# A streaming encoder layer: output products take the PSUM bank released longest ago, and the last but one row tile is scaled around the last add

## The chip, the cores and the metric

The kernel runs on one core of a Trainium2 chip. The core has five engines that run side by side, each with its own queue of instructions, done in order: TensorE (PE in the profile, with its weight loads as PEld), VectorE (DVE), ScalarE (ACT), GpSimd (POOL) and SyncE (SP, which here only issues DMAs). Matmuls write into PSUM, which is cut into banks; VectorE and ScalarE read the banks and so empty them. The metric is the device time of one execution in microseconds (us), as the median of several runs; lower is better.

## What is computed

One inference step of a hybrid encoder with one layer: 2048 prompt frames of one stream and 64 frames of a running stream, width 1024. The input is normalised and projected by one matrix into an attention part and a gated recurrent part. Their outputs stand side by side (`mix`, 1024 wide) and go through the output projection, the residual add and a last RMSNorm. The change touches only this end:

```python
y = x + jnp.concatenate([o_a, o_b], axis=-1) @ w_out   # mixer_layer
...
y_prompt = rms_norm(hp, ln_f_g)
y_sample = rms_norm(hs, ln_f_g)
```

`rms_norm(x, g)` is x times 1/sqrt(mean(x*x) + 1e-6) of its row, times g.

## The kernel before

**Tiles.** The 2048 prompt rows are worked through in four stretches of 512 (`SUPER`; the second has the 64 running frames as well). For each, the 32 column tiles of the input projection are multiplied (`project`), and attention and recurrence work on what comes out. Their result is written to DRAM (`mixd`). At the end comes the output projection. It takes 256 rows at a time: a **pair** of two row tiles of 128 (tile 0 and tile 1), eight pairs, numbered 0 to 7. Each row tile has two halves of 512 columns.

**Products.** For a pair, the product of 256 x 1024 by 1024 x 1024 is done with a Strassen-like scheme of 7 products (`NPROD`) of blocks of 128 rows by 512 by 512. Operands are split into a high and a low part, so each product is 12 matmuls of 128 x 512 into one PSUM bank: for each of 4 blocks of the inner dimension high by high, low by high, high by low (`out_step`, matmuls issued by the helper `mm` at line 249). The left operand of a product is made in `out_parts` (line 1751, ScalarE: the high part) and `out_low` (line 1759, VectorE, for pairs 0 and 1 mostly GpSimd: the low part); it lies in a `slot`, or in a part of `xh` and `xl`, which serve as a fifth slot. The sums of blocks that later products need are made at lines 1772 and 1777. The right operand, the weights, lies in memory that other stages have left: product 0 in `b11h`, `b11l`; 1 and 2 in `w`; 3 and 4 in `xh`, `xl`; 5 in `kd`, `q`, `ql`; 6 in `ph`, `v`. So a matmul's row in the profile tells its product: `acc<-w,slot` is product 1 or 2, written to the bank `acc`.

**Adds.** When a product is done, `out_adds` empties its bank. Products 0, 2 and 4 go also into a running sum `u` (`reset` or `asb`; ScalarE at line 1865, VectorE at line 1873). `ADDS` lists to which half of which tile a product is added; `out_add` does it on VectorE (line 1847), and for the sums `u` on GpSimd (line 1852). The tiles hold the residual x beforehand, in whatever buffer is free: `xn`, `bias`, two `pr`, or `rest` and `sga`. For pair 7, tile 0 is `bias` and tile 1 is two `pr`. Product 6 is added to half 0 of tile 1 alone, and it is the last add of a pair.

**Norm.** When a half has had its last add, `out_norm` squares and sums it (ScalarE, line 1896). The first half of a tile leaves its sum (line 1903), the second completes it (lines 1915 and 1916: the row factor `rstd`). Then the tile is multiplied by `rstd` and the gain `g_in` and goes out by DMA: in most tiles in one instruction (lines 1921, 1924), else by halves (lines 1937, 1940). For pair 7's tile 1 one half has been multiplied by the gain ahead (line 1909), so that ScalarE can scale it (1928, DMA at 1929) while VectorE scales the other (1931, DMA at 1932).

**Order.** Nothing on the chip chooses the order. At build time a planner (`Plan`) runs a clock of its own with estimated durations; each piece of work is a generator that yields what it waits for (a time, a free engine, a condition), and instructions get into the engines' queues in the order in which the generators go on. Tokens (`Tok`, in `tk`) count buffers: each holds planned release times; `n` is how many lie in the past, `take` removes the earliest, `when` tells it. The real waits for data and buffers are semaphores that are put in from the tiles that instructions use.

**Banks.** `out_bank` picks the bank of a product: `acc` (two buffers) or `g` (one), and when attention is over (`late`) also `tr` (two) and `pv` (one). Before the change it takes the first tag in this order that has a released buffer; the buffers of one tag are taken in turn.

## Time and profile before

| | |
|---|---|
| median of 3 runs | 1247.02 us (1246.3 to 1247.69) |
| the profiled execution | 1245.85 us, of which its span (first to last instruction) is 1244.1 us |
| PE busy | 1229.7 us of the span |
| DVE, ACT, POOL busy | 897.0, 680.6, 415.2 us |
| granted TensorE clock, mean | 0.998 |
| output stage without attention beside it | about 1098 us to the end |

How to read it: the profile page gives sums and shares; views of the trace give single instructions. A row of the timeline has start, duration, engine, line, operation, output<-inputs, shape, count, and in brackets how long the engine was idle just before it and what ended that. A row of the waits names who waited for whom, with total, count and longest. A row of the windows has the stretch, its length, the busy time of PE, PEld, DVE, ACT and POOL, the granted clock, the DMA engines' busy share and GB/s. Matmuls are pipelined: a matmul's duration is longer than the distance to the next one's start.

### The profile page before, as it was taken

What the parts mean: (1) busy time and instruction counts of PE and PEld (TensorE: products, weight loads), DVE (VectorE), ACT (ScalarE), POOL (GpSimd) and SP (SyncE); (2) the same over time, 40 slices, a digit from 0 to 9 for tenths busy, and PEclk for the clock granted to TensorE, in tenths of its full rate; (3) what the DMA queues carried; (4) which work ended last, traced back from release to release, by engine and by line L of the source; (5) the groups of instructions that cost most, each with busy time, mean ns of one, the idle gap of its engine ahead of it and who ended that gap; (6) DMA issues with size and microseconds to landing.
All of it is one profiled execution on the core that took longest, in us unless ns stands there. A gap on an engine that the chain in (4) does not pass through costs nothing.

```text
span 1244.1 us, 21258 instructions
## 1 busy us (share of the span) xinstructions
PE 1229.7 (99%) x7398; PEld 1078.0 (87%) x7398; DVE 897.0 (72%) x1897; ACT 680.6 (55%) x1526; POOL 415.2 (33%) x702
## 2 busy tenths in 40 slices
PE   9999999999999999999999999999999999999997
PEld 7888888999999999998888888988888888778785
DVE  7697878867767677786577667775768666867774
ACT  6354545754656556574465656664646445644433
POOL 7665564111120110201233242143252203665453
PEclk9999999999999999999999999999999999999999
DMA  8897888667575575655787778678888776976431
GB/s 338 302 322 258 320 297 324 204 184 255 155 217 148 158 248 189 203 164 187 276 272 247 277 265 280 226 254 264 262 280 244 238 243 208 366 243 213 144 118 68
DMA packets 158324, 294.36 MB, mean 237 GB/s; under 512 B 51657, under 2 KB 98377, under 8 KB 140554
## 3 DMA queue, kind: packets, MB, share of 16 engines
q1 hardware_dynamic: 157784, 292.74, 70.3%
q8 instruction: 58, 0.95, 0.3%
q14 instruction: 48, 0.39, 0.1%
q10 hardware_dynamic: 434, 0.27, 0.1%
HBM read 198.52 MB, written 95.49 MB: 236 GB/s over the span
## 4 chain that ended last, share of the span: by engine, by line
PE 87%; DMA 4%; DVE 4%; issue 2%; ACT 2%; POOL 1%; SPq 0%; DVEq 0%; POOLq 0%; ACTq 0%
PE acc L249 62%; PE g L249 7%; PE pv L249 6%; PE tr L253 5%; PE s L249 5%; DMA w<-wd 1%; DMA out_dram<-ck 1%; DMA way<-vT 1%; POOL sig L1777 1%; DMA vT<-way 1%; DMA mixd<-ob 1%; PE g L253 1%; DMA mixd<-mixa 0%; DMA bias<-wind 0%; DVE xn L1847 0%
## 5 line engine op out<-in xcount | busy, mean ns | idle before, releaser
L249 PE MATMUL acc<-xh,w 128*128 128x512 f32 (+2 forms) x2720 | 564.3, 347 | 0.7 <-ACT xh L409 0.5
L249 PEld LDWEIGHTS acc<-xh,w 128*128 128x128 f32 x2720 | 435.5, 189 | 51.5 <-ACT xh L409 0.9
L249 PE MATMUL acc<-xl,w 128*128 128x512 f32 (+2 forms) x1360 | 291.3, 346 | 0.4 <-DVE xl L415 0.4
L249 PEld LDWEIGHTS acc<-xl,w 128*128 128x128 f32 x1360 | 220.5, 189 | 26.3 <-DVE xl L415 0.6
L948 DVE CUSTOM_DVE_ANT_0 pr<-s,bias 128x640 f32<-128x640 f32 (+4 forms) x128 | 94.2, 736 | 52.1 <-PE s L249 51.6
L965 ACT ACTIVATE pr<-pr,nm 128x640 f32<-128x640 f32 (+4 forms) x132 | 100.3, 760 | 52.4 <-DVE nm L948 52.1
L977 ACT CAST ph<-tr 128x512 fp32r<-128x512 f32 (+3 forms) x176 | 87.8, 506 | 74.1 <-PE pv L249 45.2
L473 POOL TENSOR_TENSOR w<-wraw,w 128x256 fp32r<-128x256 f32 x120 | 102.3, 882 | 55.2 <-DVE w L468 43.2
L980 DVE TENSOR_TENSOR ph<-tr,ph 128x512 fp32r<-128x512 f32 (+3 forms) x176 | 100.8, 588 | 21.5 <-ACT ph L977 20.9
L249 PE MATMUL pv<-ph,v 128*128 128x256 f32 (+2 forms) x344 | 97.7, 370 | 0.8 <-DVE ph L980 0.5
L253 PE MATMUL tr<-ident,pr 128*128 128x128 f32 x580 | 88.3, 273 | 0.0
L1596 POOL TENSOR_TENSOR k<-ob 128x512 f32<-128x512 f32 (+2 forms) x20 | 18.0, 902 | 200.7 <-ACT ob L1587 161.7
L1121 POOL TENSOR_TENSOR mixa<-mixa,sga 128x256 f32<-128x256 f32 (+1 forms) x36 | 28.5, 793 | 167.8 <-DVE mixa L1019 154.2
L510 POOL TENSOR_TENSOR xn<-wraw,xn 128x256 fp32r<-128x256 f32 x48 | 40.2, 838 | 132.7 <-ACT xn L507 132.7
L969 DVE TENSOR_SCALAR pr<-pr,sm 128x640 f32<-128x640 f32 (+4 forms) x132 | 76.2, 577 | 4.7
L1019 DVE TENSOR_TENSOR mixa<-mixa,pv 64x256 f32<-64x256 f32 (+1 forms) x144 | 56.8, 395 | 31.0 <-ACT mixa L1015 27.3
L253 PEld LDWEIGHTS tr<-ident,pr 128*128 128x128 f32 x580 | 69.6, 140 | 10.0 <-DVE ph L980 0.8
L575 ACT ACTIVATE sig<-acc 128x512 f32<-128x512 f32 (+2 forms) x63 | 31.8, 505 | 72.2 <-PE acc L249 71.6
L249 PEld LDWEIGHTS pv<-ph,v 128*128 128x128 f32 (+1 forms) x344 | 58.3, 189 | 9.5 <-DVE ph L980 1.2
L1015 ACT COPY mixa<-pv 64x256 f32<-64x256 f32 (+1 forms) x72 | 25.1, 349 | 59.2 <-PE pv L249 53.4
L249 PE MATMUL s<-kd,q 128*128 128x320 f32 (+2 forms) x232 | 55.9, 311 | 0.2 <-DVE nm L948 0.2
L249 PE MATMUL s<-kd,ql 128*128 128x320 f32 (+2 forms) x232 | 55.5, 309 | 0.0
(343 smaller groups left out, 2124.1 us busy)
## 6 DMA issues: line engine op xcount, KB each, us to landing
w<-wd SPq DMA_DIRECT2D x96, 1024.0 KB, 5.9
wd<-w SPq DMA_DIRECT2D x32, 1024.0 KB, 7.0
wraw<-in_w_in_dram SPq DMA_DIRECT2D x30, 512.0 KB, 5.4
wod<-xn SPq DMA_DIRECT2D x28, 512.0 KB, 5.7
xn<-in_x_prompt_dram SPq DMA_DIRECT2D x23, 512.0 KB, 4.6
bias<-biasd SPq DMA_DIRECT2D x24, 320.0 KB, 5.7
carry<-kd SPq DMA_DIRECT2D x12, 512.0 KB, 6.6
carry<-v SPq DMA_DIRECT2D x12, 512.0 KB, 6.6
```

The source lines that it names most:

```text
L249: pe.matmul(out, w, x, **kw)
L253: pe.transpose(out, x, idn)
L473: pool.tensor_sub(w[:, 1, k : k + 2], raw[:, k : k + 2], f32(w[:, 0, k : k + 2]))
L510: pool.tensor_sub(f32r(st[:, c.start + 512 : c.stop + 512]), src[:, c], st[:, c])
L575: act.activation(sig[:, :bn], acc, AF.Exp, scale=-1.0)
L948: dve.tensor_tensor_reduce(s[:, :nk].rearrange("p (a c) -> p a c", a=ns), sps[:, :ns, :kn], d.bias[:, h, bcol : bcol + nk].rearrange("p (a ...
L965: act.activation(s[:, :nk], s[:, :nk], AF.Exp, bias=nm[:, 0:1], scale=-1.0, accum_out=sm)
L969: dve.tensor_scalar(s[:, :nk], s[:, :nk], sm, None, ALU.mult)
L977: act.copy(ph[:krows, 0, :wid], pt[:krows, :wid])
L980: dve.tensor_sub(ph[:krows, 1, :wid], pt[:krows, :wid], f32(ph[:krows, 0, :wid]))
L1019: dve.tensor_add(mix[hs, :qn], mix[hs, :qn], pv[hs, i, :qn])
L1121: pool.tensor_mul(mix[:, :n], mix[:, :n], d.sg[:, g0 : g0 + n])
```

## The change

Two things. First, `out_bank` takes, of the tags that have a released buffer, the one whose buffer was released earliest by the planner's times, in place of the first in a fixed order. Second, for the last add of all (pair 7, product 6) `out_adds` waits until the first half of tile 0 has been scaled, and the scaling of tile 0's second half waits until that add has been issued, in place of waiting for a planned time; in both halves the DMA is issued to SP's queue at once.

```diff
@@ out_bank
-        tag = [x for x in some if tk[x].n][0]
+        tag = min((x for x in some if tk[x].n), key=lambda x: tk[x].when())
@@ out_adds
+        closing = i == len(pairs) - 1 and k == NPROD - 1
         for tile_, half in ADDS[k]:
+            if closing:
+                yield lambda: "scaled0" in o
             t = yield from out_add(o, tile_, half, bank[1], t)
+        if closing:
+            o["added"] = True
@@ out_norm
                 c = slice(a * 512, a * 512 + 512)
-                yield "D", t
+                if end and a:
+                    yield lambda: "added" in o
+                else:
+                    yield "D", t
                 dve.scalar_tensor_tensor(x[a][:rows], x[a][:rows], r[:rows], g_in[:rows, c], ALU.mult, ALU.mult)
                 t = C.dve(530, t)
-                yield t
+                if end:
+                    o["scaled0"] = True
+                else:
+                    yield t
                 sp.dma_start(y[:, c], x[a][:rows])
```

## The prediction

> **What bounds the kernel.** First the page: which engine is full.

> ```profile
> PE 1229.7 (99%) x7398; PEld 1078.0 (87%) x7398; DVE 897.0 (72%) x1897; ACT 680.6 (55%) x1526; POOL 415.2 (33%) x702
> ```

> TensorE is busy 99% of the span, so an edit that touches no matmul can only win back holes in its row and the stretch behind its last matmul. The first part of the change deals with the PSUM bank that an output product takes, so I ask the waits of PE from 1098 us, where attention has ended, to 1236 us, the last matmul.

> ```profile
> PE acc L249 <- DVE pr L1847: 1.5, 2, 0.9
> PE acc L249 <- DVE xn L1847: 0.9, 2, 0.5
> ```

> The columns are total, count and longest. All four waits of this stage are for line 1847, the add that empties a bank. Everything the first part can win is here. Next the timeline of PE around each of the four.

> ```profile
> 1109.87 0.39 PE L249 MATMUL acc<-v,slot 128*128 128x512 f32 x1
> 1110.71 0.47 PE L249 MATMUL acc<-b11h,xh 128*128 128x512 f32 x1 [0.46 <-DVE xn L1847]
> ...
> 1113.52 2.88 PE L249 MATMUL acc<-w,slot 128*128 128x512 f32 x12
> 1117.30 3.34 PE L249 MATMUL acc<-w,slot 128*128 128x512 f32 x12 [0.89 <-DVE pr L1847]
> 1120.48 0.61 PE L249 MATMUL acc<-xh,slot 128*128 128x512 f32 x2
> ...
> 1179.64 0.39 PE L249 MATMUL acc<-b11l,slot 128*128 128x512 f32 x1
> 1180.67 3.01 PE L249 MATMUL acc<-w,slot 128*128 128x512 f32 x12 [0.64 <-DVE pr L1847]
> 1183.52 2.88 PE L249 MATMUL g<-w,slot 128*128 128x512 f32 x12
> 1186.24 0.39 PE L249 MATMUL acc<-xh 128*128 128x512 f32 x1
> ...
> 1218.74 0.39 PE L249 MATMUL acc<-b11l,slot 128*128 128x512 f32 x1
> 1219.53 3.00 PE L249 MATMUL acc<-w,slot 128*128 128x512 f32 x12 [0.40 <-DVE xn L1847]
> 1222.37 2.88 PE L249 MATMUL g<-w,slot 128*128 128x512 f32 x12
> ```

> An undisturbed product is 12 matmuls in 1186.24 - 1183.52 = 2.72 us, 0.227 us from start to start. Against that pace the real loss is more than the idle time in brackets, because the first matmul behind a hole is slow too. Site 1 (product 0 of pair 2): due at 1109.87 + 0.23 = 1110.10, starts at 1110.71, and its 12 take 2.81: 0.61 + 0.09 = 0.70 us. Site 2 (product 2 of pair 2): due at 1116.24, starts at 1117.30, takes 3.18: 1.06 + 0.46 = 1.52. Site 3 (product 1 of pair 5): due at 1179.87, starts at 1180.67, takes 2.85: 0.80 + 0.13 = 0.93. Site 4 (product 1 of pair 7): due at 1218.97, starts at 1219.53, takes 2.84: 0.56 + 0.12 = 0.68. Together 3.83 us.

> **Part one: the bank.** It adds no instruction. In the planner a bank is taken at once when any has been released, before and after; taking the oldest leaves as many released banks at every later moment, so I expect the same order of instructions on every engine with other bank names. Two buffers of `acc`, one of `g`, two of `tr` and one of `pv` make six banks in the late stage; taken in turn, a bank comes back some six products, about 16 us, later. What must be asked at each site is what PE meets next once the bank is free.

> ```profile
> 1114.80 1.76 DVE L1921 SCALAR_TENSOR_TENSOR bias<-bias,rstd,gin 128x1024 f32<-128x1024 f32 x1
> ...
> 1116.48 0.67 DVE L1847 TENSOR_TENSOR pr<-pr,acc 128x512 f32<-128x512 f32 x1
> ...
> 1117.08 0.68 DVE L1759 TENSOR_TENSOR slot<-sga,slot 128x512 fp32r<-128x512 f32 x1
> ...
> 1117.81 2.40 PEld L249 LDWEIGHTS acc<-w,slot 128*128 128x128 f32 x11 [0.35 <-DVE slot L1759]
> ```

> At site 2 the second matmul of the product loads the low half of its operand, which DVE makes at line 1759 from 1117.08 to 1117.76; the load starts at 1117.81 and names it. DVE works without a gap in front of it (1.76 us of row scaling, then the add), so that time doesn't move. With a free bank PE does one matmul early and then stands at the second till the same 1117.81. What site 1 gains, 0.70, is also spent there. **Sites 1 and 2 together: nothing.** The bounds are 0 and all of their 2.22 us; I take 0, since the row that holds PE is in the trace.

> ```profile
> 1179.84 0.69 DVE L1847 TENSOR_TENSOR pr<-pr,acc 128x512 f32<-128x512 f32 x1 [1.27 <-POOL pr L1852]
> 1180.44 0.68 DVE L1759 TENSOR_TENSOR slot<-vT,slot 128x512 fp32r<-128x512 f32 x1
> ...
> 1218.70 0.69 DVE L1847 TENSOR_TENSOR xn<-xn,acc 128x512 f32<-128x512 f32 x1 [1.25 <-POOL xn L1852]
> 1219.30 1.28 DVE L1759 TENSOR_TENSOR slot<-vT,slot 128x512 fp32r<-128x512 f32 x2
> ```

> Sites 3 and 4 are alike: the last add of the pair before waits for GpSimd's last add into the same half tile, and the bank is held meanwhile. The low halves queued behind that add are for product 2, not for the waiting product 1. At site 3 product 2 would then begin at 1179.87 + 2.72 = 1182.59; its low half ends at 1181.12, 1.5 us ahead. At site 4, with both gains in, product 2 would begin at 1222.37 - 0.68 - 0.93 = 1220.76; its low half ends by 1219.98 even if GpSimd's chain doesn't move at all, 0.8 us ahead. **Sites 3 and 4: 0.93 + 0.68 = 1.61 us**, bounds 0 (the next wait takes it all) and 1.61. No PE wait stands between them or behind them to the last matmul, so what is won reaches the end.

> **Part two: the end.** Timeline of the last microseconds of work.

> ```profile
> 1235.32 0.20 ACT L1916 ACTIVATE rstd<-rstd 128x1 f32<-128x1 f32 x1
> ...
> 1235.77 0.39 PE L249 MATMUL acc<-v,slot 128*128 128x512 f32 x1
> 1236.25 0.69 DVE L1847 TENSOR_TENSOR pr<-pr,acc 128x512 f32<-128x512 f32 x1 [1.38 <-issue]
> 1236.86 0.74 DVE L1937 SCALAR_TENSOR_TENSOR bias<-bias,rstd,gin 128x512 f32<-128x512 f32 x1
> ...
> 1238.29 0.75 DVE L1931 SCALAR_TENSOR_TENSOR pr<-pr,rstd,gin 128x512 f32<-128x512 f32 x1 [0.69 <-ACT rstd L1916]
> 1238.96 0.75 DVE L1937 SCALAR_TENSOR_TENSOR bias<-bias,rstd,gin 128x512 f32<-128x512 f32 x1
> 1239.04 0.37 ACTq L1929 DMA_DIRECT2D out_dram<-pr  x1
> 1239.10 0.33 SPq L1932 DMA_DIRECT2D out_dram<-pr  x1
> 1239.53 1.27 SPq L1940 DMA_DIRECT2D out_dram<-bias  x2
> ```

> The last but one row tile is `bias` here, the last one `pr`. DVE is idle for 1.38 us ahead of the last add. The scale of `bias` is ready at 1235.52 (1235.32 + 0.20), so its first half can start at about 1235.56. DVE lets the next instruction start 0.67 us behind such a scale (1238.29 to 1238.96), so the last add can start at 1236.23; it starts at 1236.25 now. The move costs nothing as long as that cover of 0.02 us holds; without it the end is late by as much as the scale is, and 0.67 of that (a whole scale) is in the low end of this term. The second half follows at 1236.84 and ends near 1237.6, inside the time in which DVE waits for the last tile's factor (till 1238.29). Behind the scale on DVE stand only the add, the second half and line 1931; on SP only the three output DMAs, which leave in a new order: the two of `bias` at about 1236.4 and 1237.7, then line 1932 at 1239.10 as now. They take SP 0.33 us each and are gone by then. Nothing is removed or added; two DMAs move 2 to 3 us earlier.

> What is that worth? The windows of the last microseconds, whose last two columns are DMA share and GB/s:

> ```profile
> 1239.80:1240.20 0.40, 0.00 (x0) 0.00 (x0) 0.00 (x0) 0.00 (x0) 0.00 (x0) 0.50 0.71 271
> 1240.20:1240.60 0.40, 0.00 (x0) 0.00 (x0) 0.00 (x0) 0.00 (x0) 0.00 (x0) 0.50 1.01 384
> ...
> 1242.60:1243.00 0.40, 0.00 (x0) 0.00 (x0) 0.00 (x0) 0.00 (x0) 0.00 (x0) 0.50 0.16 56
> ```

> All four 256 KB outputs go out in one burst with every DMA engine full at 384 GB/s, from about 1239.9 to 1242.65; the span ends 1.45 us behind it. With two gone ahead, 0.52 MB remain, 1.37 us at 384 GB/s, and the burst ends near 1241.3. The landing times give nearly the same (the issue of the second `bias` DMA; the median us to landing of the two; the times of all output DMAs from 1190 us on):

> ```profile
> 1240.01 0.80 SPq L1940 DMA_DIRECT2D out_dram<-bias  x1
> ```

> ```profile
> out_dram<-bias SPq DMA_DIRECT2D x2, 256.0 KB, 3.0
> ```

> ```profile
> DMA to landing us min/median/max: 2.0/2.6/3.1
> ```

> Now the last lands at about 1240.0 + 3.0 = 1243.0; then it is line 1932's, 1239.10 + 2.6 = 1241.7. **The end: 1.3 us**, bounds 0.6 (the add delayed by its 0.67) and 1.4.

> **Sum:** 0 + 1.61 + 1.3 = 2.9 us. The profiled execution took 1245.85 (span 1244.1), 1.2 below the median shown; taken off that median, 1247.02 - 2.9 = **1244.1 us**. The runs before spread by 0.7 either way, and a measurement of this kernel tells about 0.2%, 2.5 us, from no change; the forecast is just beyond that.

> **Rivals.**

> *All four bank waits go* (chance 0.09). It needs the low half at site 2 to come earlier or PE not to stand there: 3.83 + 1.3 = 5.1, 1241.9 us. For it: all four waits name a bank. Against it: the weight load at 1117.81. [...]

> *Another wait takes the banks' place at sites 3 and 4* (0.12). A low half of line 1759, or a hi half, turns out late by 0.8 to 1.5 us: only the end is won, 1245.7 us. Against it: the margins above. That the oldest bank isn't the free one on the chip, because the planner's release times are not the chip's, ends here too; but six banks in turn leave some 16 us.

> *The end gives nothing* (0.11). The scale comes later than the last add or the burst isn't what ends the span: 1.6 won, 1245.4 us. For it: the cover on DVE is 0.02 us.

> *The clock falls: slower* (0.08). The rows of the granted clock (seventh column) behind the last matmul:

> ```profile
> 1238.70:1239.20 0.50, 0.00 (x0) 0.00 (x0) 0.50 (x2) 0.31 (x1) 0.00 (x0) 0.95 0.00 0
> 1239.20:1239.70 0.50, 0.00 (x0) 0.00 (x0) 0.50 (x1) 0.00 (x0) 0.00 (x0) 0.50 0.00 0
> ```

> PE ends at 1236.16, and 0.95 over half a microsecond puts the fall at 1239.15: 3.0 us of idle PE halved the clock. At site 2 the two holes become one: PE would stand from about 1115.8 to 1117.8, 2.0 us. At half clock a product takes 2.72 us more. One such product leaves no gain, and from two on the kernel is slower; three give 3 x 2.72 - 2.9 = +5.3, 1252.3 us. Against it: 2.0 is less than 3.0, and the holes of today left the clock whole. [...]

> **Chances and range.** Forecast 0.60. About a fifth of it falls short of 2.5 us by the run's spread: 0.47 faster, 0.13 same. With the first rival 0.56 faster; with the second and third 0.36 same; the fourth, 0.08, slower. The range reaches down to the first rival, 1241.8, and up to the second and the third with the spread of the runs on top, 1245.7 + 0.7 = 1246.4; it leaves out the clock.

> **What would show it.** In the profile after, products of the late stage write `tr`, `pv`, `g` and `acc` in turn, and PE has no wait for line 1847. The second matmul of product 2 of pair 2 still waits for line 1759, with a longer wait. The distance from that point to the last matmul, now 1236.16 - 1117.81 = 118.35, is 116.7. The first half at line 1937 runs ahead of the last add; the add starts within 0.15 us of the last matmul's end; two `bias` DMAs land before line 1931; the final burst is half as long, and the span ends 6.6 us behind the last matmul instead of 7.9. I would be wrong if a wait of 0.5 us or more stood at sites 3 or 4, if the order of other instructions had changed, or if any window of the stage showed a clock under 1.

## The result, and the profile after

The changed kernel takes **1243.44 us** (median of 14 runs, 1242.46 to 1245.78), the one before 1246.72 in the same comparison (14 runs, 1245.49 to 1248.39). The ratio is 0.9977, with a 95% interval of 0.9969 to 0.9985: 1.9 to 3.9 us are gone, 3.3 by the medians. The profiled execution of the changed kernel took 1244.75 us, its span is 1243.0, the mean granted clock 0.997.

The page first, the row of the busy times after the change:

```profile
PE 1229.9 (99%) x7398; PEld 1079.5 (87%) x7398; DVE 896.0 (72%) x1897; ACT 680.2 (55%) x1526; POOL 415.7 (33%) x702
```

The instruction counts are those of before: nothing was added or removed. The two profiled spans are only 1.1 us apart, though, and that is less than the medians say. A span holds the whole execution, and this kernel comes to its output stage at another time in every profile. So I cut each span at four points that can be read off the timeline of PE: the start of the last product of pair 1, the start of product 4 of pair 2 (both lie around sites 1 and 2), the end of the last matmul, and the end of the span.

| us | stage begins | to product 4 of pair 2 | to the last matmul's end | to the span's end |
|---|---|---|---|---|
| before | 1107.35 | 15.85 | 112.96 | 7.9 |
| after | 1107.76 | 17.46 | 111.14 | 6.6 |
| difference | +0.41 | **+1.61** | **-1.82** | **-1.3** |

The last column is rounded because spans are given to 0.1 us. The last two stretches give 3.1 us; the first of the stage takes half of it back in this execution. Each in turn, beginning with the waits of PE from 1098 to 1236 us, after the change (total, count, longest):

```profile
PE acc L249 <- DVE slot L1759: 1.8, 1, 1.8
```

All waits for line 1847 are gone, and one wait for the low half at line 1759 stands instead. The timeline of PE around sites 1 and 2, after:

```profile
1110.51 0.40 PE L249 MATMUL pv<-b11h,xh 128*128 128x512 f32 x1
...
1113.25 2.88 PE L249 MATMUL g<-w,slot 128*128 128x512 f32 x12
1115.97 0.48 PE L249 MATMUL acc<-w,slot 128*128 128x512 f32 x1
1118.24 3.89 PE L249 MATMUL acc<-w,slot 128*128 128x512 f32 x11 [1.79 <-DVE slot L1759]
1121.93 1.05 PE L249 MATMUL acc<-xh,slot 128*128 128x512 f32 x2
...
1125.22 0.61 PE L249 MATMUL tr<-xh,slot 128*128 128x512 f32 x2
```

```profile
1118.24 3.17 PEld L249 LDWEIGHTS acc<-w,slot 128*128 128x128 f32 x11 [2.10 <-DVE slot L1759]
```

Product 0 of pair 2 begins without a wait, in `pv`, and so does product 2, at 1115.97. One matmul of it runs, and then PE stands till the low half is there: 1.79 us in PE's own row, 2.10 in that of the weight loads. So far this is as forecast. What wasn't forecast is the pace behind it. Eleven matmuls take 3.89 us where e1 below needs 2.79. The windows of that stretch, after (the granted clock is the third figure from the end):

```profile
1118.00:1119.00 1.00, 0.76 (x3) 0.67 (x4) 1.00 (x3) 0.00 (x0) 0.00 (x0) 1.00 0.88 340
1119.00:1120.00 1.00, 1.00 (x5) 0.77 (x4) 1.00 (x3) 0.00 (x0) 0.00 (x0) 0.82 0.83 205
1120.00:1121.00 1.00, 1.00 (x3) 0.79 (x3) 1.00 (x2) 0.72 (x2) 0.00 (x0) 0.50 0.80 254
...
1123.00:1124.00 1.00, 1.00 (x5) 0.83 (x5) 0.56 (x1) 0.00 (x0) 1.00 (x1) 0.97 1.01 362
...
1126.00:1236.00 110.00, 110.00 (x486) 89.90 (x484) 78.96 (x122) 45.72 (x116) 55.09 (x63) 1.00 0.41 129
```

The clock fell to one half. A mean of 0.82 over 1 us puts 0.36 us of it at half speed, 0.97 puts 0.06 there, and three whole windows lie between: 3.42 us, from 1119.64 to 1123.06. (The row of one of the three stands here; the other two show 0.50 as well.) As an estimate from that, 3.42 us at half speed do 1.71 us of work, so about 1.7 us are lost; the table shows 1.61. PE looks busy all the while, 1.00 in the row of 1120 to 1121 at a clock of 0.50: in a busy share a slow clock isn't seen. The last row is the rest of the stage, without a fall.

Sites 3 and 4, after, each with the last matmul ahead of it:

```profile
1181.45 0.39 PE L249 MATMUL pv<-b11l,slot 128*128 128x512 f32 x1
1181.68 2.88 PE L249 MATMUL g<-w,slot 128*128 128x512 f32 x12
...
1219.63 0.39 PE L249 MATMUL acc<-b11l,slot 128*128 128x512 f32 x1
1219.86 2.88 PE L249 MATMUL acc<-w,slot 128*128 128x512 f32 x12
```

Both follow 0.23 us behind the matmul ahead, the pace of an undisturbed product. The end, timeline after:

```profile
1235.52 0.20 ACT L1921 ACTIVATE rstd<-rstd 128x1 f32<-128x1 f32 x1
...
1235.75 0.75 DVE L1945 SCALAR_TENSOR_TENSOR bias<-bias,rstd,gin 128x512 f32<-128x512 f32 x1 [0.68 <-ACT rstd L1921]
1235.97 0.39 PE L249 MATMUL acc<-v,slot 128*128 128x512 f32 x1
1236.46 0.69 DVE L1847 TENSOR_TENSOR pr<-pr,acc 128x512 f32<-128x512 f32 x1
1236.53 1.67 SPq L1951 DMA_DIRECT2D out_dram<-bias  x2
...
1237.06 0.75 DVE L1945 SCALAR_TENSOR_TENSOR bias<-bias,rstd,gin 128x512 f32<-128x512 f32 x1
...
1239.31 0.33 SPq L1937 DMA_DIRECT2D out_dram<-pr  x1
```

The first half of `bias` is scaled ahead of the add, the second right behind it, and the add starts 1236.46 - 1236.36 = 0.10 us behind the last matmul; before it was 0.09. The last windows after (DMA share and GB/s at the end of the row), and the landing times:

```profile
1240.00:1240.40 0.40, 0.00 (x0) 0.00 (x0) 0.00 (x0) 0.00 (x0) 0.00 (x0) 0.50 0.69 266
...
1241.20:1241.60 0.40, 0.00 (x0) 0.00 (x0) 0.00 (x0) 0.00 (x0) 0.00 (x0) 0.50 0.77 282
```

```profile
out_dram<-bias SPq DMA_DIRECT2D x2, 256.0 KB, 2.0
...
out_dram<-pr SPq DMA_DIRECT2D x1, 256.0 KB, 2.8
```

The burst that ran from 1239.9 to 1242.65 now runs from about 1240.1 to 1241.5. The two `bias` outputs land in 2.0 us instead of 3.0, ahead of it.

### The profile page after: what moved, and what is told of

The parts are those of the page before. It is cut to its first block, busy times and chain, and to the rows that moved or that the text cites. A ratio compares the mean times of both kernels' runs of the same rounds, so it can differ in the third digit from the quotient of the medians.

```text
span 1243.0 us, 21228 instructions
## 1 busy us (share of the span) xinstructions
PE 1229.9 (99%) x7398; PEld 1079.5 (87%) x7398; DVE 896.0 (72%) x1897; ACT 680.2 (55%) x1526; POOL 415.7 (33%) x702
## 4 chain that ended last, share of the span: by engine, by line
PE 92%; DMA 4%; DVE 3%; ACT 1%; issue 0%; SPq 0%; DVEq 0%; ACTq 0%
PE acc L249 61%; PE g L249 9%; PE pv L249 7%; PE tr L253 6%; PE s L249 5%; PE tr L249 3%; DMA out_dram<-ck 1%; DMA way<-vT 1%; DMA vT<-way 1%; PE g L253 1%; DMA w<-wd 0%; DMA mixd<-mixa 0%; DMA lbg<-in_lb_gamma_dram 0%; DMA bias<-wind 0%; ACT ck L1901 0%
## 5 line engine op out<-in xcount | busy, mean ns | idle before, releaser
L249 PE MATMUL acc<-xh,w 128*128 128x512 f32 (+2 forms) x2720 | 564.2, 347 | 0.8 <-ACT xh L409 0.7
L249 PEld LDWEIGHTS acc<-xh,w 128*128 128x128 f32 x2720 | 435.4, 189 | 51.6 <-ACT xh L409 0.9
L249 PE MATMUL acc<-xl,w 128*128 128x512 f32 (+2 forms) x1360 | 291.4, 346 | 0.5 <-DVE xl L415 0.5
L249 PEld LDWEIGHTS acc<-xl,w 128*128 128x128 f32 x1360 | 220.5, 189 | 26.5 <-DVE xl L415 0.7
L249 PE MATMUL pv<-ph,v 128*128 128x256 f32 (+2 forms) x344 | 97.7, 370 | 0.9 <-DVE sm L968 0.7
L249 PEld LDWEIGHTS pv<-ph,v 128*128 128x128 f32 (+1 forms) x344 | 58.3, 189 | 9.4 <-ACT pr L965 1.1
L249 PE MATMUL s<-kd,q 128*128 128x320 f32 (+2 forms) x232 | 55.8, 311 | 0.2 <-DVE nm L948 0.2
L249 PE MATMUL s<-kd,ql 128*128 128x320 f32 (+2 forms) x232 | 55.5, 309 | 0.0
```

The lines of the kernel that those rows point to most:

```text
L249: pe.matmul(out, w, x, **kw)
```

## The experiments

The theory was: sites 1 and 2 become one wait of unchanged end, worth nothing; the fall of the clock is a separate thing that the longer gap brings about in some executions; sites 3 and 4 and the end give what they are worth. The expectations call this theory 'gap and clock'; in its rival 'the gap alone' the fall has nothing to do with the gap. The other rivals were that turning through six banks itself costs clock, and that the bank rule costs something at site 2 in every execution. Each diff is against the kernel that is named.

**e1: the bank rule alone**, against before.

```diff
-        tag = [x for x in some if tk[x].n][0]
+        tag = min((x for x in some if tk[x].n), key=lambda x: tk[x].when())
```

> The bank rule alone, the end as before. Both theories: from product 4 of pair 2 to the end of the last matmul 111.1 us as after the change (before 113.0), from the last matmul's end to the end of the span 7.9 us as before. [...] Median 1.0 to 1.9 us faster than before. [...]

Median 1245.38 us (11 runs); ratio to before 0.9987 (0.9977 to 0.9997). Timeline of PE in e1:

```profile
1118.61 2.79 PE L249 MATMUL acc<-w,slot 128*128 128x512 f32 x11 [1.79 <-DVE slot L1759]
...
1123.96 0.61 PE L249 MATMUL tr<-xh,slot 128*128 128x512 f32 x2
```

The gap is the same 1.79 us, but the eleven matmuls behind it take 2.79: the clock held, 1.00 in every window. The stretch to product 4 is 15.83 us, 15.85 before. So sites 1 and 2 are worth nothing here, 0.02 us, and the +1.61 of the table is the clock and not the rule. The next stretch is 111.14, the end 7.9.

**e2: the end alone**: the changed kernel with the old line in `out_bank`.

```diff
-        tag = min((x for x in some if tk[x].n), key=lambda x: tk[x].when())
+        tag = [x for x in some if tk[x].n][0]
```

> The order at the end alone, the banks as before. All four waits of PE for line 1847 are back and the clock stays at 1.00 up to the last matmul. From the last matmul's end to the end of the span 6.6 us (before 7.9). Theory 'the burst of outputs': 1.3 us faster in the median. Rival 'the end is set by something fixed behind the outputs': within 0.3 us of before.

Median 1245.80 (11 runs); ratio 0.9987 (0.9978 to 0.9995). The waits of PE from 1098 to 1236 us in e2:

```profile
PE acc L249 <- DVE pr L1847: 1.7, 2, 0.9
PE acc L249 <- DVE xn L1847: 0.9, 2, 0.5
```

All four are back; the stretches are 15.81, 113.09 and 6.7. The two parts are independent: the middle stretch follows the bank rule, the last one the order at the end.

**e3: the gap filled**: the changed kernel, with eight matmuls ahead of product 2 of pair 2.

```diff
         bank = yield from out_bank()
+        if (i, k) == (2, 2):
+            fill = s_ps()[:, 0]
+            for _ in range(8):
+                pe.matmul(fill, m[0][:, 0], w(0, 0), start=True, stop=True)
```

> As after the change, with eight more matmuls into an unused bank ahead of product 2 of pair 2; they use operands that are ready and their result is not read, so they fill most of the 2 us in which PE waits there. Theory 'gap and clock': the clock stays at 1.00 through the stage in every execution, from the low half's load to product 4 it takes 5.4 us, and the median is 0.3 to 1.6 us below that of the change, by how often the clock falls there without them. Rival 'the gap alone' (the fall has nothing to do with the gap): the same median as the change, 2.9 us below before, and a fall is as likely as without them.

Median 1244.16 (12 runs); ratio 0.9975 (0.9967 to 0.9984). The row of weight loads behind the filler in e3:

```profile
1120.54 1.46 PEld L249 LDWEIGHTS acc<-w,slot 128*128 128x128 f32 x7 [0.38 <-DVE slot L1759]
```

Of the 2.10 us of waiting 0.38 are left, the clock is 1.00, and the stretch is 15.85: filling costs nothing and the low half stays what sets the time. In the median e3 can't be told from the change, whose interval of 0.9969 to 0.9985 overlaps. Were the fall in every execution, e3 should lie 1.6 us, or 0.0013 of the ratio, below the change; it lies 0.0002 below. The intervals are too wide to decide this by the medians (each reaches 0.0008 or more to either side); that the fall isn't in every execution is shown by the profiles, of e1 first.

**e4: the low half first**: the changed kernel; one row tile's scaling on VectorE waits until product 2's low half has been issued.

```diff
         if x[3] is not None and not end:
+            if tile_ and o is outp.get(1):
+                yield lambda: (2, 2) in a_at
             yield "D", t
```

> As after the change, with the row scale of tile 1 of pair 1 put behind the low half of product 2 of pair 2 on VectorE. Theory 'VectorE's order makes the gap': the low half is ready 1.2 to 1.6 us earlier, PE's wait there shrinks from 2.1 us to under 0.9, the clock stays at 1.00, and the kernel is 1.3 to 1.6 us faster than the change where the clock does not fall and up to 3 where it does: 4.2 to 5.5 us below before. Rival 'another wait follows at once' (a later low half or add that the scale now delays): the gain is given back within the next two products, and the median is within 0.5 us of the change.

Median 1243.72 (7 runs); ratio 0.9972 (0.9961 to 0.9982). PE's wait in the stage falls to 0.3 us, and the stretch to product 4 is 14.33, 1.50 less than in e1, with the others unchanged (111.14, 6.7). This is what confirms the reading of site 2: putting the low half ahead of one row scaling on VectorE moves PE, where freeing the bank didn't. The median is less clear than the trace: it lies 3.6 us below before, less than the 4.2 to 5.5 that were expected, and next to e3 the gain is 0.44 us. Part of the reason is that each execution of this kernel takes 2.0 to 2.2 us outside its span (the same in e7), where the change, e1 to e3 and e6 take 1.7 to 1.8; by the medians of the spans the gain on e3 is 0.75 us. Why this edit costs some 0.35 us outside the span stays open.

**e5: the gap longer**: the changed kernel with the subtraction of line 1759 three times for this product.

```diff
-            (pool if e == "P" else dve).tensor_sub(m[1][:, c], src[:, c], f32(m[0][:, c]))
+            for _ in range(3 if (i, k) == (2, 2) else 1):
+                (pool if e == "P" else dve).tensor_sub(m[1][:, c], src[:, c], f32(m[0][:, c]))
```

> As after the change, with the subtraction that makes the low half of product 2 of pair 2 done three times over (the same result each time), so that PE's wait there grows from 2.1 to about 3.3 us. Theory 'gap and clock': the fall is now all but certain; the clock shows 0.5 for 3 us or more behind the gap, and from the low half's load to product 4 it takes 6.5 to 7.2 us. Rival 'the gap alone': the clock stays at 1.00 and that stretch takes 5.4 us.

One run of 1247.96 us. Timeline of PE and windows of e5:

```profile
1121.36 4.38 PE L249 MATMUL acc<-w,slot 128*128 128x512 f32 x11 [3.24 <-DVE slot L1760]
...
1128.32 0.62 PE L249 MATMUL tr<-xh,slot 128*128 128x512 f32 x2
```

```profile
1121.00:1122.00 1.00, 0.64 (x2) 0.53 (x3) 1.00 (x3) 0.00 (x0) 0.00 (x0) 0.80 1.10 205
1122.00:1123.00 1.00, 1.00 (x3) 0.76 (x3) 1.00 (x2) 0.00 (x0) 0.00 (x0) 0.50 0.81 295
...
1125.00:1126.00 1.00, 1.00 (x5) 0.83 (x5) 0.23 (x1) 0.18 (x1) 0.00 (x0) 0.99 1.07 334
```

A gap of 3.24 us brings the fall again, 0.2 us after PE resumed: 0.40 + 3 + 0.02 = 3.42 us at half speed. From the low half's load to product 4 it is 1128.32 - 1121.36 = 6.96 us, and 1125.22 - 1118.24 = 6.98 in the profile of the change; in e1, without a fall, 1123.96 - 1118.61 = 5.35. A fall costs 1.6 us at both gaps.

**e6: the changed kernel again** (no edit), to see whether its clock falls each time.

> The changed kernel once more, on the chip and in the rounds of the next one. Theory 'gap and clock': a gap of 2.1 us, a fall in some executions only (one of two profiles with this gap showed it); from the last product of pair 1 to product 4 of pair 2 it takes 15.8 us without a fall and 17.5 with one. Rival 'the gap alone': 15.8 us, no fall. Both: 111.1 us from product 4 of pair 2 to the last matmul's end, 6.6 behind it, and 2.5 to 3.5 us below before.

Median 1244.65 (11 runs); ratio 0.9979 (0.9971 to 0.9988). Timeline of PE in e6:

```profile
1119.26 2.83 PE L249 MATMUL acc<-w,slot 128*128 128x512 f32 x11 [1.21 <-DVE slot L1759]
```

No fall: the clock is 1.00 and the stretch 15.28. But the gap was shorter too, 1.21 us against 1.79, in a kernel with not one instruction changed. So this doesn't tell whether the longer gap brings the fall each time.

**e7: e4's kernel again** (no further edit), on the chip of e6.

> The kernel with the row scale behind the low half, beside the change on the same chip. From the last product of pair 1 to product 4 of pair 2 14.3 us and no fall. Theory 'VectorE's order makes the gap': 1.5 to 2.3 us below the change in the median. Rival 'another wait follows': within 0.5 us of it.

Median 1242.81 (5 runs, 1241.59 to 1243.06); ratio 0.9964 (0.9951 to 0.9978). Timeline of PE in e7:

```profile
1116.35 2.81 PE L249 MATMUL acc<-w,slot 128*128 128x512 f32 x11 [0.31 <-DVE slot L1759]
...
1121.71 0.62 PE L249 MATMUL tr<-xh,slot 128*128 128x512 f32 x2
```

The stretch is 14.35. Its median lies 1.84 us below e6's on the same chip. The intervals of the two ratios still overlap, but the slowest of the 5 runs (1243.06) is faster than the fastest of the 11 of e6 (1243.61), the trace names the place, and twice gave the same 14.3 us: the kernel of e4 and e7 is better than the change.

**e8: the changed kernel, one more profile** (no edit).

> One more profile of the changed kernel, for how often the clock falls. Theory 'gap and clock': either no fall and 15.8 us from the last product of pair 1 to product 4 of pair 2, or a clock of 0.5 near 1120 us and up to 17.5. Rival 'the gap alone': no fall.

One run of 1243.99 us; gap 1.2, clock 1.00, stretch 15.23: e6's case once more. What makes the gap 1.2 or 1.8 us long can be read from VectorE and GpSimd ahead of it. First the profile of the change, VectorE then GpSimd:

```profile
1113.44 1.86 DVE L1926 SCALAR_TENSOR_TENSOR xn<-xn,rstd,gin 128x1024 f32<-128x1024 f32 x1
1115.22 1.76 DVE L1926 SCALAR_TENSOR_TENSOR bias<-bias,rstd,gin 128x1024 f32<-128x1024 f32 x1
...
1117.51 0.68 DVE L1759 TENSOR_TENSOR slot<-sga,slot 128x512 fp32r<-128x512 f32 x1
```

```profile
1113.48 2.42 POOL L1777 TENSOR_TENSOR wraw<-wraw,sga 128x256 f32<-128x256 f32 x2
```

And the same instructions in e8:

```profile
1114.92 1.27 DVE L1926 SCALAR_TENSOR_TENSOR xn<-xn,rstd,gin 128x1024 f32<-128x1024 f32 x1
...
1116.41 1.46 DVE L1926 SCALAR_TENSOR_TENSOR bias<-bias,rstd,gin 128x1024 f32<-128x1024 f32 x1 [0.22 <-ACT rstd L1921]
```

```profile
1114.96 3.50 POOL L1777 TENSOR_TENSOR wraw<-wraw,sga 128x256 f32<-128x256 f32 x2
```

Either VectorE is the slow one (1.86 and 1.76 us, GpSimd's pair 2.42) or GpSimd (3.50, VectorE 1.27 and 1.46). Before, the change, e1 to e5 are of the first kind, e6, e8 and e9 of the second, and in e7, too, the first scaling takes 1.27. The chip alone doesn't decide it: e5 and e6 ran on the same one. With the order of e4 it no longer matters, 14.33 us in the first kind and 14.35 in e7. There is no profile of before of the second kind, so the 0.02 us of sites 1 and 2 are shown for the first kind alone.

**e9: e5 with the longer gap filled** by 13 matmuls.

```diff
+        if (i, k) == (2, 2):
+            fill = s_ps()[:, 0]
+            for _ in range(13):
+                pe.matmul(fill, m[0][:, 0], w(0, 0), start=True, stop=True)
```

> The kernel with the subtraction done three times over, with 13 matmuls into an unused bank ahead of product 2 of pair 2, 2.9 us of PE work whose result is not read. VectorE does the same as in the longer gap, but PE no longer stands. Theory 'gap and clock' (PE's idle time is the cause): the clock stays at 1.00, and from the last product of pair 1 to product 4 of pair 2 it takes 17.0 us. Rival 'the extra work on VectorE or the late operand does it': a clock of 0.5 again and 18.9 us.

One run of 1242.74 us. Timeline of PE and windows of e9:

```profile
1114.58 3.23 PE L1834 MATMUL s<-w,slot 128*128 128x512 f32 x13
1117.65 2.88 PE L249 MATMUL acc<-w,slot 128*128 128x512 f32 x12
```

```profile
1118.00:1119.00 1.00, 1.00 (x6) 0.82 (x5) 1.00 (x3) 0.00 (x0) 0.00 (x0) 1.00 1.41 180
...
1120.00:1121.00 1.00, 1.00 (x6) 0.84 (x5) 1.00 (x3) 0.61 (x3) 0.00 (x0) 1.00 0.97 389
```

VectorE does the same work as in e5, but PE never stands, and the clock stays at 1.00; the stretch is 16.72 instead of 18.89. By this pair, one profile each, it is PE's idleness that brings the fall, and neither VectorE's extra work nor the bank rule, which e5 and e9 share. How much of the 2.17 us between the two is the clock's can't be read from them alone, as e9 is of the second kind of VectorE's timing: 1.6 by the rows above.

**How often the clock falls** isn't measured well. With a gap of 1.8 us it fell in one profile of two, with 1.2 in neither of two, with 3.24 in the only one; the last section has what the traces show of it. For the executions without a trace there is only a mean clock, rounded: it is 0.997 in 6 of 37 executions of kernels with the gap (after, e1, e6, e8) and in 1 of 83 of before, e2, e3, e4, e7 and e9. That is a coarse marker, for e5 fell and shows 0.998. Taken as it is, one execution in six falls, about 1.6 / 6 = 0.3 us on average.

## Why the prediction was right, and where not

The forecast was 2.9 us less, 1244.1; the medians say 3.3 less, 1243.44. The 2.9 lies inside the interval of 1.9 to 3.9, and the terms are those that were named. With the clock whole, the stretches give 0.02 (e1) + 1.82 + 1.3 = 3.1 us, less about 0.3 for the fall. Two things that the sum lacked, a fifth bank wait (+0.2) and the clock (-0.3), nearly cancel; that the total is so near is in part luck. The distance from the low half of site 2 to the last matmul, forecast as 116.7, came out as 1236.36 - 1118.24 = 118.12; in e1, without the fall, it is 1235.10 - 1118.61 = 116.49.

- **Sites 1 and 2, nothing: right, shown by e1** (15.83 against 15.85, both of the first kind of VectorE's timing). The low half at site 2 keeps its time and PE waits for it, 1.8 us instead of 0.35. e4 shows the other side: an earlier low half gives 1.50. The rival in which all four waits go fell there. Turning through the banks did close every bank hole in these traces, but closing a hole is worth something only where nothing else stands behind it, three places of five.
- **Sites 3 and 4, 1.61: right in the mechanism, too small by 0.2.** The stretch gave 1.82. The rest is a fifth bank wait that I overlooked, since I asked for the waits of PE's own row alone. It stands among the weight loads, before the change:

```profile
1154.26 0.19 PEld L249 LDWEIGHTS acc<-xh,slot 128*128 128x128 f32 x1 [0.37 <-DVE xn L1847]
```

PE's row has no idle time at this place: the row ahead of it ends at 1153.23 + 1.09 = 1154.32, behind the start of the waiting matmul at 1154.26. The timeline of PE before and then after the change, at the same two products:

```profile
1153.23 1.09 PE L249 MATMUL g<-w,slot 128*128 128x512 f32 x4
1154.26 0.50 PE L249 MATMUL acc<-xh,slot 128*128 128x512 f32 x1
1154.60 0.39 PE L249 MATMUL acc<-xl,slot 128*64 128x512 f32 x1
```

```profile
1154.33 2.00 PE L249 MATMUL acc<-w,slot 128*128 128x512 f32 x8
1156.17 0.40 PE L249 MATMUL tr<-xh,slot 128*128 128x512 f32 x1
1156.41 0.39 PE L249 MATMUL tr<-xl,slot 128*64 128x512 f32 x1
```

Before, the waiting matmul starts 0.35 us behind the one ahead of it (1153.23 + 3 x 0.227 = 1153.91), and the next one 0.34 behind it; after, they are 0.23 (1156.17 - 1155.94, where 1155.94 is 1154.33 + 2.00 - 0.39) and 0.24. That is the missing 0.2 us. The wait that was to take the banks' place didn't come.

- **The end, 1.3: right** (1.3; e1 and e2 show that it comes from this part alone). The cover on VectorE was just enough: the add starts 0.10 us behind the last matmul. The two outputs landed early, the burst is half as long.
- **The clock: the mechanism was named as a rival, but the argument against it failed.** "2.0 is less than 3.0" was the argument that the one long hole at site 2 would leave the clock whole. It didn't: 1.79 us sufficed in one profile. The 3.0 was how long PE had been idle at the kernel's end when the clock fell; it isn't a least gap, and what counts isn't the length of a gap alone, as 1.79 us left the clock at 1.00 in e1 (last section). The price of three products at half clock was also off: 3.42 us at half speed cost 1.6. So the fall stays below the 3.1 us won, even in an execution that has it, and the sign couldn't turn. The sign I had named for being wrong (a window of the stage with a clock under 1) did appear.
- **The turn through six banks cost no clock**, 1.00 over 110 us of it, and it took idle time of PE away: from 1126 to 1236 us PE was busy for 110.00 us, before for 108.96.

## What to carry to other kernels

Before counting a wait as a gain, read what the engine's next instruction waits for: four holes named a bank, and what the first two could give was all taken by one late operand. Two small holes pushed together into one can even cost time: behind 1.79 us of idle PE in one profile of two, and behind 3.24 us in e5, the clock stood at 0.50 for 3.42 us and 1.6 us were lost. Fill such a hole with spare matmuls or, better, bring the late operand forward. And transfers that can leave before the last work are worth taking out of the final burst: half a megabyte taken ahead gave 1.3 us, with not one instruction less.

## What the hardware showed that I had not expected

**The clock fell after PE had resumed, and both falls in the stage lasted 3.42 us.** In the profile of the change PE resumed at 1118.24 and the clock fell at 1119.64; in e5 it resumed at 1121.36 and the clock fell at 1121.60. In the change the idle time was shorter than the fall: the 3.41 us ahead of the fall, from 1116.23 on, hold the idle time from 1116.45 to 1118.24 entire, and that is 52% of them.

| profile | step | PE idle in it | clock behind it |
|---|---|---|---|
| e5, gap | 1118.19 to 1121.60 | 93% | 0.50 |
| before, end of the kernel | 1235.73 to 1239.15 | 87% | 0.50 |
| the change, end of the kernel | 1235.69 to 1239.11 | 80% | 0.50 |
| the change, gap | 1116.23 to 1119.64 | 52% | 0.50 |
| e6, gap | any 3.41 us | at most 35% | 1.00 |
| before, sites 1 and 2 | 1116.27 to 1119.68 | 27% | 1.00 |
| the change, ahead of the stage | 1020.66 to 1024.07 | 21% | 1.00 |

The three falls of before and of the change have a step of 52% or more ahead of them, and no other step of these two traces, up to the fall at the end, is above 27%. At which share between 35% and 52% the clock begins to fall was not shown. As an estimate from these numbers, if the grid lies anywhere with equal chance, a gap of 1.79 us falls wholly into one step in (3.41 - 1.79) / 3.41 = 47% of executions, and is shared by two in the others. That may be what tells e1, with its 1.79 us and a clock of 1.00, from the change; where e1's gap lay on the grid was not shown. No run moved a gap on the grid on purpose, and how often the gap is 1.8 us and not 1.2 stays open.

**Of VectorE and GpSimd side by side one takes longer, and which of them isn't fixed.** With GpSimd idle the scaling of a whole row tile of `xn` takes VectorE 1.28 and 1.29 us (the change, at 1104.60 and 1107.89). In the change and in e8 such a scaling and GpSimd's pair start 0.04 us apart, VectorE's first, and one time VectorE pays (1.86 us for 1.27), the other time GpSimd (3.50 for 2.42). The order of the starts is the same in both, so what decides here stays open. A difference of 0.6 us at the same place in two profiles of one kernel can be just this.
